# Weight sums of a Strassen product in six stages, a tile of its own for the first product, output weights in halves, and earlier requests for the reload and the first heads

## The chip, the cores and the metric

The kernel runs on one core of one Trainium2 chip. A core has TensorE (PE, matrix products), VectorE (DVE), ScalarE (ACT), GpSimd (POOL) and SyncE (SP, which mostly issues transfers), each with its own instruction stream that it works off in order, and DMA engines that move data between the chip's memory and the core's buffers. The engines wait for each other by semaphores. The metric is the device time of one execution in microseconds (us); lower is better.

## The reference

What is computed is one layer of a diffusion transformer: 2048 tokens on a grid 64 wide, and 256 context tokens, 1024 values each. One wide projection gives queries, keys, values and gates of a neighbourhood attention and of a retention; their gated results go through an output projection.

```python
def reference(x, c, ctx, c_ctx, norm_g, w_ada, b_ada, w_in, na_rpb, ret_decay_fwd,
              ret_decay_bwd, ret_norm_g, w_out, final_norm_g):
...
        mod = jax.nn.silu(c) @ w_ada[i] + b_ada[i]
...
        shift, scale, gate = mod[:, None, :D], mod[:, None, D:2 * D], mod[:, None, 2 * D:]
...
        h_lat = _rmsnorm(x, norm_g[i]) * (1.0 + scale) + shift
        h_ctx = _rmsnorm(ctx, norm_g[i]) * (1.0 + scale_c) + shift_c
...
        y_lat, y_ctx = _mixer(h_lat, h_ctx, w_in[i], na_rpb[i], lg_f, lg_b, ret_norm_g[i],
                              w_out[i], update_ctx)
        x = x + gate * y_lat
...
    return _rmsnorm(x, final_norm_g)
```

`_mixer` begins with the products `h @ w_in` (1024 x 4096) and ends with `@ w_out` (1024 x 1024). The kernel scales `w_out` by `gate` beforehand, and so has the gated sum from one product.

All values are float32. A product of float32 matrices is made of three TensorE products of rounded parts: each operand is cut into a high part (`whi`, `hhi`: a cast to the type `fp32r`, on ACT) and a low part (`wlo`, `hlo`: the rest, by a subtraction on POOL or VectorE), and high x high, high x low and low x high are summed in PSUM.

## The kernel before

The tokens of `h` are four blocks of 512 columns (`blk[0]` to `blk[3]`), each kept as a high and a low tile; the context is `blk[4]`. The kernel runs through these stages on TensorE:

1. Five windows (`window(b)`, products on line L354): the attention's keys for the four token blocks and the context. The norm and the cutting of the blocks run beside them, by a table of steps, `PLAN`: an entry is the step of a window, the action and its arguments. The actions `'w'` and `'w2'` request the raw weights of the first two context products (four DMAs of `w_in` into the staging tile `st`, issued by SP on L176).
2. Units of the context (six of 48 products, L365) and values of blocks 0 and 1 (`values`, eight units of 48).
3. The first Strassen region: queries and gates of blocks 0 and 1. Each of six sets (`SETS`) takes a weight of 1024 x 256 and makes four outputs by seven products instead of eight (`w_set`; each product, `prod` on L625, is 12 matmuls of 512 columns). The products are called by their weight: A11, A12, S4, A22, S2, S3, S1. Sums of quarters of the weight (`s1` to `s4`) and of the blocks (`t1` to `t4`) are made beforehand.
4. Values of blocks 3 and 2, and the second region for these blocks. The two blocks' tiles were stored to memory (`spill_step`, L487) and are loaded back (`reload_parts`, L771).
5. A lead of 192 products for the retention's values, beside which the first head of the attention is loaded; then attention (L944 and on), retention and output projection, which the change leaves alone.

The weight's sums are written in `w_sums`: a list of functions, one for each of the four steps of the set before (`step(n)` calls `ahead[n]`). `cut` makes one part: a cast on ACT (L579) and a subtraction on POOL (L580); the sums are VectorE's (L587 to L590 and L595). In `w_set`, ACT copies the first product to half of tile `o3` (L653), since VectorE adds it to the second (L654) and to S2's (L660). `o3` is one tile with no second buffer, and its other half is an output that a DMA stores (`fin` and `store`, L150; `gS`, `ggS` and `qS` are the stored gates and queries). PSUM holds six tiles for the products, handed out in the order in which they come free.

In the gaps of the regions runs the preparation of the output weight, called from a list of `hooks`, four for a set. `wo_gate(k)` adds one piece of `w_ada` into the row `gacc` (L690) and requests the next 512 KB (`wraw`, L687), `wo_row` turns the row into all partitions by two matmuls (L697), and `wo_mul(k)` multiplies one eighth of `w_out` by it (L701), cuts it (ACT L705, POOL L706) into two tiles `g` and stores four pieces to `woS` one step later, from ACT's queue (L708). `load_w` requests the raw weight for the next sum (L176), and `w_split` cuts a whole weight (ACT L336, POOL or VectorE L338).

At the lead's beginning SP has `load_w`, and after it the first head's loads: `load_head` (`k<-kS`), `load_q` and `load_v` (`vt<-vB`).

## Time and profile before

| what | us |
|---|---|
| time, median of three | 1449.82 |
| lowest and highest | 1444.53, 1451.17 |
| profiled execution | 1451.75 |
| its span in the profile | 1450.0 |
| mean granted TensorE clock | 0.969 of full speed |

The page of the profile gives busy time for each engine and the span in 40 slices of 36 us. Digits are tenths busy; PEclk is the clock granted to TensorE.

```profile
PE   6989899889898787789999999999999999999997
...
DVE  5686147455576343427776777777663544444445
ACT  5454232233223233236555645555563133333332
POOL 4352244434335545335553534446443144544442
PEclk9999899999989898999999999999999999999999
```

TensorE is at 7 to 9 tenths in the slices of 165 to 650 us (the 5th to the 18th digit), where the change lies, and at 9 or more behind. A row of a timeline reads: start, length, engine, line, operation, what it writes from what it reads, and in brackets the idle time of that engine before it and what ended it. `SPq` and `ACTq` are SP's and ACT's queues, where a DMA is issued.

### The profile page before, as it was taken

Reading aid. Unit: us, or ns where it says so; the run is one execution under the profiler, and the core shown is the slowest. Engines: PE = TensorE matmul, PEld = TensorE weight load, DVE = VectorE, ACT = ScalarE, POOL = GpSimd, SP = SyncE. Lnnn points to the kernel's source line nnn. Section 1 sums busy time; section 2 is a strip of 40 time slices with the busy share of each in tenths; the row PEclk is TensorE's granted clock in tenths of the full one; section 3 lists DMA queues with packets and bytes.
Section 4 is the critical chain, followed back from the end, with each engine's and each line's share of the span. In section 5 each row is a group of like instructions: output and inputs, shape, how many; then the busy total and the mean of one; then the engine's idle time right before and its main releaser. Section 6 shows DMA issues by size and latency. Waiting matters only on the chain.

```text
span 1450.0 us, 23128 instructions
## 1 busy us (share of the span) xinstructions
PE 1338.7 (92%) x8236; PEld 1167.1 (80%) x8236; DVE 828.2 (57%) x1426; ACT 589.1 (41%) x1239; POOL 620.9 (43%) x585
## 2 busy tenths in 40 slices
PE   6989899889898787789999999999999999999997
PEld 2467799667697666679889988998999879888886
DVE  5686147455576343427776777777663544444445
ACT  5454232233223233236555645555563133333332
POOL 4352244434335545335553534446443144544442
PEclk9999899999989898999999999999999999999999
DMA  9448664577684645488677779988555898655533
GB/s 317 149 160 290 224 198 109 167 270 226 251 300 112 213 130 183 172 237 233 183 180 211 204 204 270 278 213 219 167 149 171 246 298 267 200 183 166 162 117 124
DMA packets 231765, 295.64 MB, mean 204 GB/s; under 512 B 17633, under 2 KB 172385, under 8 KB 230626
## 3 DMA queue, kind: packets, MB, share of 16 engines
q1 hardware_dynamic: 200322, 237.79, 55.7%
q10 hardware_dynamic: 31328, 56.37, 10.9%
q8 instruction: 66, 1.08, 0.3%
q14 instruction: 49, 0.40, 0.1%
HBM read 196.57 MB, written 97.52 MB: 203 GB/s over the span
## 4 chain that ended last, share of the span: by engine, by line
PE 44%; DMA 5%; DVE 4%; issue 3%; POOL 3%; ACT 2%; SPq 0%; ACTq 0%; POOLq 0%; DVEq 0%
PE mm L1383 10%; PE mm L365 10%; PE sS L944 5%; PE mm L354 4%; PE tr L971 3%; PE po L992 3%; PE tr L973 2%; PE po L994 2%; PE mm L1106 2%; DMA v<-rvS 1%; DMA k<-kS 1%; PE mm L1295 1%; PE mm L1294 1%; PE mm L1293 1%; PE mm L1274 1%
## 5 line engine op out<-in xcount | busy, mean ns | idle before, releaser
L365 PE MATMUL mm<-whi,hhi 128*128 128x256 f32 x768 | 226.8, 295 | 0.7 <-DMA hhi<-hS 0.5
L365 PE MATMUL mm<-whi,hlo 128*128 128x256 f32 x768 | 219.2, 285 | 4.3 <-DMA hlo<-hS 4.3
L365 PE MATMUL mm<-wlo,hhi 128*128 128x256 f32 x768 | 219.0, 285 | 1.7 <-POOL wlo L338 1.7
L975 ACT CAST pt<-tr 128x640 fp32r<-128x640 f32 (+1 forms) x128 | 95.7, 748 | 169.9 <-PE tr L973 167.5
L981 DVE TENSOR_TENSOR pt<-tr,pt 128x640 fp32r<-128x640 f32 (+1 forms) x128 | 114.0, 890 | 77.1 <-ACT pt L975 75.8
L365 PEld LDWEIGHTS mm<-whi,hlo 128*128 128x128 f32 x768 | 148.5, 193 | 5.4 <-DMA hlo<-hS 5.3
L964 POOL TENSOR_SCALAR sp<-sp,stt 128x640 f32<-128x640 f32 (+2 forms) x128 | 103.5, 811 | 112.9 <-DVE stt L963 77.9
L365 PEld LDWEIGHTS mm<-wlo,hhi 128*128 128x128 f32 x768 | 148.2, 193 | 2.1 <-POOL wlo L338 2.1
L365 PEld LDWEIGHTS mm<-whi,hhi 128*128 128x128 f32 x768 | 148.2, 193 | 1.7 <-ACT o L634 0.7
L625 PE MATMUL mm<-hhi,whi 128*128 128x512 f32 x336 | 107.5, 421 | 35.3 <-DVE o L660 27.5
L953 DVE CUSTOM_DVE_ANT_0 sp<-sS,nb 128x640 f32<-128x640 f32 (+2 forms) x128 | 105.6, 825 | 37.4 <-DMA nb<-in_rpb_t_dram 23.7
L338 POOL TENSOR_TENSOR wlo<-st,whi 128x256 fp32r<-128x256 f32 (+1 forms) x79 | 83.8, 1072 | 98.9 <-ACT whi L336 78.1
L958 ACT ACTIVATE sp<-sp,stt 128x640 f32<-128x640 f32 (+2 forms) x128 | 107.4, 839 | 27.6 <-DVE stt L953 26.5
L625 PEld LDWEIGHTS mm<-hhi,whi 128*128 128x128 f32 x336 | 67.4, 202 | 56.3 <-issue 30.3
L944 PE MATMUL sS<-k,q 128*128 128x256 f32 (+3 forms) x512 | 99.5, 316 | 12.4 <-DMA vt<-vB 7.0
L354 PE MATMUL mm<-hhi,whi 128*128 128x512 f32 x256 | 108.3, 423 | 0.0
L354 PE MATMUL mm<-hlo,whi 128*128 128x512 f32 x256 | 102.1, 399 | 5.8 <-DVE hlo L255 2.3
L354 PE MATMUL mm<-hhi,wlo 128*128 128x512 f32 x256 | 102.5, 400 | 0.2 <-DVE wlo L338 0.2
L580 POOL TENSOR_TENSOR whi<-st,whi 128x512 fp32r<-128x512 f32 x48 | 66.4, 1404 | 78.3 <-ACT whi L579 51.5
L944 PEld LDWEIGHTS sS<-k,q 128*128 128x128 f32 x512 | 83.6, 190 | 18.7 <-DVE stt L953 7.7
L1383 PE MATMUL mm<-wor,y 128*128 128x512 f32 x384 | 95.6, 398 | 1.3 <-DVE xt L1392 1.2
L1392 DVE TENSOR_TENSOR xt<-mm,xt 128x512 f32<-128x512 f32 x64 | 43.8, 687 | 85.0 <-PE mm L1383 79.5
(254 smaller groups left out, 3116.2 us busy)
## 6 DMA issues: line engine op xcount, KB each, us to landing
st<-in_w_in_dram SPq DMA_DIRECT2D x64, 512.0 KB
q<-qS SPq DMA_DIRECT2D x64, 256.0 KB
k<-kS SPq DMA_DIRECT2D x16, 576.0 KB
kS<-o SPq DMA_DIRECT2D x16, 512.0 KB
hS<-hhi SPq DMA_DIRECT2D x16, 512.0 KB
hS<-hlo SPq DMA_DIRECT2D x16, 512.0 KB
vB<-o SPq DMA_DIRECT2D x64, 128.0 KB
qS<-o ACTq DMA_DIRECT2D x16, 512.0 KB
```

The costliest lines, as they stand in the source:

```text
L338: eng.tensor_tensor(l, r, f(h), ALU.subtract)
L354: nc.tensor.matmul(pm[:, :n], ww[:, k, cs], h[:, k, :], start=(k == 0 and i == 0), stop=(k == KC - 1 and i == 2))
L365: nc.tensor.matmul(pm[:, t * WG:(t + 1) * WG], h[:, k, o:o + P], ww[:, k, :], start=(k == 0 and i == 0), stop=(k == KC - 1 and i == 2))
L580: nc.gpsimd.tensor_tensor(t[:, 1], r, f(t)[:, 0], ALU.subtract)
L625: nc.tensor.matmul(pm, ww[:, k, :], hh[:, k, :], start=(k == 0 and i == 0), stop=(k == KH - 1 and i == 2))
L944: nc.tensor.matmul(o, hd["q"][i][:, hl, j * P:(j + 1) * P], k, start=(hl == 0), stop=(hl == 1))
L953: nc.vector.tensor_tensor_reduce(T["sp"][:, :n], T["s"], nbz[big][:, o:o + n], -1.0, 3e38, ALU.add, ALU.min, T["st"][:, 0:1])
L958: nc.scalar.activation(sp[:, :n], sp[:, :n], AF.Exp, bias=st[:, 0:1], scale=-1.0, accum_out=st[:, 1:2])
L964: nc.gpsimd.tensor_scalar(sp[:, :n], sp[:, :n], st[:, 2:3], 0.0, ALU.mult, ALU.add)
L975: nc.scalar.copy(pt[:, :ng_ + 2, 0, :], tr[:, :ng_ + 2, :])
L981: nc.vector.tensor_tensor(pt[:, :n, 1, :], tr[:, :n, :], f(pt)[:, :n, 0, :], ALU.subtract)
L1383: nc.tensor.matmul(pm, yy[:, k, :], ww[:, k, sl], start=(k == 0 and i == 0), stop=(k == 3 and i == 2))
```

## The change

It has seven parts:

- `PLAN`: the action `'w2'` (the second context weight) moves from step 106 to the end of window 3 (127).
- `w_sums`: four stages become six. The sums stand a stage after the first cuts, `a22` is cut a stage ahead of `s4`, `s3` ahead of `s2`, `s1` alone, and `load_w` last. Stages 0 to 3 run in the set before, stages 4 and 5 in the set's own first two steps (`mine[4 + n:5 + n] + ahead[n:n + 1]`), and `values` calls stages 0 to 2 after units 4, 5 and 6 and stage 3 at its end.
- `w_set`: the first product goes to the tile `e` (of the pool `wo["p"]`, one buffer), which also takes the sum `u3`; no DMA reads it. `o3` is first written at S2. After S1 the sum for `o3` comes first, and its `fin` too.
- `wo_open` runs ahead of the first region, `wo_gate(k)` at hooks 3k + 2 for k up to 6, `wo_gate(7)` after unit 1 of the second values, and `wo_row` after unit 7.
- `wo_mul(k, n)` does half n of piece k, at hook 3k + n, with a tile `g` of one buffer in place of two; the next load comes after the second half.
- The reload of blocks 3 and 2 is requested at hooks 20 and 21 (the first two steps of the region's last set).
- `load_w` stands behind the first head's loads.

```diff
-    (90, 'cs', 8), (92, 'rs', 8), (94, 'hl', 7, 0), (95, 'hl', 7, 1), (96, 'sp', 8), (106, 'w'), (106, 'w2'),
-    (108, 'mu', 8, 1), (108, 'ab', 8, 1), (109, 'hl', 8, 1), (114, 'mu', 8, 0), (117, 'ab', 8, 0), (127, 'hl', 8, 0),
+    (90, 'cs', 8), (92, 'rs', 8), (94, 'hl', 7, 0), (95, 'hl', 7, 1), (96, 'sp', 8), (106, 'w'),
+    (108, 'mu', 8, 1), (108, 'ab', 8, 1), (109, 'hl', 8, 1), (114, 'mu', 8, 0), (117, 'ab', 8, 0), (127, 'hl', 8, 0), (127, 'w2'),
...
         def p0():
             cut("a11", 0, 0, a11)
             cut("a12", 0, 1, a12)
+
+        def p1():
             V(a11, a11, a21, ALU.subtract)
             V(a12, a12, a22, ALU.subtract)
             V(a12, a12, a11, ALU.add)
             V(a21, a21, a22, ALU.add)
-
-        def p1():
+            cut("a22", 1, 1, a22)
+
+        def p2():
             cut("s4", 1, 0, a12)
-            cut("a22", 1, 1, a22)
             V(a22, a22, a11, ALU.subtract)
 
-        def p2():
+        def p3():
+            cut("s3", 2, 1, a11)
             cut("s2", 2, 0, a22)
-            cut("s3", 2, 1, a11)
-
-        def p3():
+
+        def p4():
             cut("s1", 3, 0, a21)
-            load_w()
-
-        return W, [p0, p1, p2, p3]
+
+        return W, [p0, p1, p2, p3, p4, load_w]
...
-        (oa, (_, xa)), (ob, (yb, xb)) = out_tile(), out_tile(True)
-        nc.scalar.copy(yb, prod(W["a11"], b11))
-        V(xa, prod(W["a12"], b21), yb, ALU.add)
+        et = wo["p"].tile([P, 2, 512], F32, name="e")
+        s1, u3 = (lay(et[:, e, :]) for e in range(2))
+        oa, xa = out_tile()
+        nc.scalar.copy(s1, prod(W["a11"], b11))
+        V(xa, prod(W["a12"], b21), s1, ALU.add)
         step(0)
         m3 = prod(W["s4"], b22)
         fin(oa, 0, A)
         m4 = prod(W["a22"], t4)
         step(1)
-        V(xb, prod(W["s2"], t2), yb, ALU.add)
-        V(yb, prod(W["s3"], t3), xb, ALU.add)
+        ob, xb = out_tile(True)
+        V(xb, prod(W["s2"], t2), s1, ALU.add)
+        V(u3, prod(W["s3"], t3), xb, ALU.add)
...
-        V(xd, m5, yb, ALU.add)
         V(xb, m5, xb, ALU.add)
+        V(xd, m5, u3, ALU.add)
+        fin(ob, 0, B)
         fin(od, 1, B)
-        fin(ob, 0, B)
         step(3)
...
-    def wo_mul(k):
-        nc.vector.tensor_tensor(wo["w"], wo["w"], wo["acc"], ALU.mult)
-        for n in range(2):
-            sl = slice(n * 512, (n + 1) * 512)
-            w = wo["p"].tile([P, 2, 512], F32R, name="g", bufs=2)
+    def wo_mul(k, n):
+        sl = slice(n * 512, (n + 1) * 512)
+        nc.vector.tensor_tensor(wo["w"][:, sl], wo["w"][:, sl], wo["acc"][:, sl], ALU.mult)
+        w = wo["p"].tile([P, 2, 512], F32R, name="g")
...
-        if k + 1 < KC:
+        if n == 1 and k + 1 < KC:
             wo_load(a["w_out"][(k + 1) * P:(k + 2) * P, :])
...
-    W = values((w0, w1), (0, 1), h_sums(T, 0, 1), None)
+    W, mine = values((w0, w1), (0, 1), h_sums(T, 0, 1), {})
+    wo_open()
+
+    def take(b):
+        for d in reload_parts(b):
+            nc.sync.dma_start(*d)
+
     hooks = [[spill_step] if n < 16 else [] for n in range(24)]
-    for n, e in enumerate([wo_open] + [g(k) for k in range(8)]):
-        hooks[2 * n + 1].append(e)
-    hooks[22].append(wo_row)
+    for k in range(7):
+        hooks[3 * k + 2].append(lambda k=k: wo_gate(k))
+    hooks[20].insert(0, lambda: take(3))
+    hooks[21].insert(0, lambda: take(2))
...
-    strassen(T, 0, 1, W, hooks, mid)
-    for b in (3, 2):
-        for d in reload_parts(b):
-            nc.sync.dma_start(*d)
+    strassen(T, 0, 1, W, mine, hooks, mid)
...
-    W = values((w0, w1), (3, 2), h_sums(T, 2, 3), None)
+    W, mine = values((w0, w1), (3, 2), h_sums(T, 2, 3), {1: lambda: wo_gate(7), 7: wo_row})
     hooks = [[] for n in range(24)]
     for k in range(8):
-        hooks[3 * k].append(m(k))
+        for n in range(2):
+            hooks[3 * k + n].append(lambda k=k, n=n: wo_mul(k, n))
...
-    load_w()
...
     heads[0] = load_head(0)
     load_q(heads[0], 0, 0)
     load_v(heads[0], (0, 1, 2))
+    load_w()
```

SP, in the last third of window 3, where the table's entry has moved; `hS` and `kS` are stores of a token block and of the keys, `st` the weight's staging tile.

```order
 L487 DMA hS_0_93<-hhi 128x1024 x2
 L150 DMA kS_61<-o 256x1x512
-L176 DMA st<-in_w_in_dram 128x4x256 x4
+L176 DMA st<-in_w_in_dram 128x4x256 x2
 L487 DMA hS_0_93<-hhi 128x1024 x2
 L150 DMA kS_62<-o 256x1x512
 L487 DMA hS_1_94<-hlo 128x1024 x2
 L150 DMA kS_63<-o 256x1x512
-L487 DMA hS_1_94<-hlo 128x1024 x2
+L487 DMA hS_1_94<-hlo 128x1024
+L176 DMA st<-in_w_in_dram 128x4x256 x2
+L487 DMA hS_1_94<-hlo 128x1024
```

Two of the four pieces now stand behind five stores of blocks and two of keys.

VectorE in one set of the first region, before; L654 adds the copy to A12's product, L595 is `a22` less `a11`, L660 takes S2's product:

```order
L654 TENSOR_TENSOR o<-mm,o_2495 128x512
L587 TENSOR_TENSOR st<-st 128x4x128
L588 TENSOR_TENSOR st<-st 128x4x128
L589 TENSOR_TENSOR st<-st 128x4x128
L590 TENSOR_TENSOR st<-st 128x4x128
L595 TENSOR_TENSOR st<-st 128x4x128
L690 SCALAR_TENSOR_TENSOR gacc<-wraw,silc,gacc 128x1024
L660 TENSOR_TENSOR o_2495<-mm,o_2495 128x512
L661 TENSOR_TENSOR o_2495<-mm,o_2495 128x512
```

and the same set now (L658 was L654, L665 was L660, L597 was L595, L695 was L690):

```order
L658 TENSOR_TENSOR o<-mm,e 128x512
L695 SCALAR_TENSOR_TENSOR gacc<-wraw,silc,gacc 128x1024
L589 TENSOR_TENSOR st<-st 128x4x128
L590 TENSOR_TENSOR st<-st 128x4x128
L591 TENSOR_TENSOR st<-st 128x4x128
L592 TENSOR_TENSOR st<-st 128x4x128
L665 TENSOR_TENSOR o_2568<-mm,e 128x512
L666 TENSOR_TENSOR e<-mm,o_2568 128x512
L668 TENSOR_TENSOR o<-mm,e 128x512
L669 TENSOR_TENSOR o_2568<-mm,o_2568 128x512
L597 TENSOR_TENSOR st<-st 128x4x128
L674 TENSOR_TENSOR o_2568<-mm,o_2568 128x512
```

The subtraction of `a22` has moved from ahead of S2's add to behind four adds, and the gate's sum from behind the weight's sums to ahead of them.

ACT in the first set of the second region, before; `g` is the cut of the output weight and `woS` its store, L639 and L150 a gate and its store, L579 a cast of the weight's sums:

```order
L653 COPY o_3652<-mm 128x512
L579 CAST whi<-st 128x512 x2
L705 CAST g<-wraw 128x512 x2
L639 ACTIVATE o<-o 128x512
L708 DMA woS_95<-g 128x512
L708 DMA woS_96<-g 128x512
L708 DMA woS_95<-g 128x512
L708 DMA woS_96<-g 128x512
L150 DMA gS_69<-o 128x512
```

and now (L657 was L653, L709 was L705, L712 was L708):

```order
L657 COPY e<-mm 128x512
L579 CAST wlo<-st 128x512
L579 CAST whi<-st 128x512 x2
L709 CAST g<-wraw 128x512
L640 ACTIVATE o<-o 128x512
L712 DMA woS_95<-g 128x512
L712 DMA woS_96<-g 128x512
L150 DMA gS_69<-o 128x512
L579 CAST wlo<-st 128x512
L709 CAST g<-wraw 128x512
L640 ACTIVATE o<-o 128x512
L712 DMA woS_95<-g 128x512
```

The second cast of `g` stands behind the stores of the first, and both write the same tile.

More of the change, by code (lines that the diff above doesn't have):

```diff
@@ L609, in p1, with w_set @@
             res.append(w_split(wcur.pop(0), lo=1))
-        return [None, p1, None, None]
-    def w_set(c0, W, T, A, B, ahead, hooks):
+        return [None, p1, None, None, None, None]
+    def w_set(c0, W, T, A, B, mine, ahead, hooks):
         isq = c0 < 512
@@ L629, in out_tile @@
             o = env["st"].tile([P, 2, 512], F32R, name="o3", bufs=1) if extra else op.tile([P, 2, 512], F32R, name="o")
-            return o, [lay(f(o)[:, e, :]) for e in range(2)]
+            return o, lay(f(o)[:, 1, :])
         def fin(o, ct, b):
@@ L644, in step @@
             tick()
-            if ahead[n]:
-                ahead[n]()
+            for fn in mine[4 + n:5 + n] + ahead[n:n + 1]:
+                if fn:
+                    fn()
             if hooks:
@@ L717, in unit, with strassen @@
             spill_step()
-    def strassen(T, A, B, W, hook, last):
+    def strassen(T, A, B, W, mine, hook, last):
         for n, c0 in enumerate(SETS):
@@ L724, in strassen, with values @@
                 Wn, ahead = last, plain_next(last)
-            w_set(c0, W, T, A, B, ahead, hook)
-            W = Wn
-    def values(ws, bb, hs, W):
-        ahead = [None] * 4
+            w_set(c0, W, T, A, B, mine, ahead, hook)
+            W, mine = Wn, ahead
+    def values(ws, bb, hs, hook):
         vu = [(w, c0, tp) for w, c0 in zip(ws, (1024, 1280)) for b in bb for tp in (2 * b, 2 * b + 1)]
@@ L738, in values @@
             if n == 4:
-                W, ahead = w_sums(wcur.pop(0))
-            if n in (4, 5):
-                ahead[n - 4]()
+                W, mine = w_sums(wcur.pop(0))
+            if n > 3 and n < 7:
+                mine[n - 4]()
+            if n in hook:
+                hook[n]()
         while hs:
             hs.pop(0)()
-        ahead[2]()
-        ahead[3]()
-        return W
+        mine[3]()
+        return W, mine
     load_w()
```

22 lines of the change are left out of this document (10 added, 12 removed).

## The prediction

> **What bounds the kernel now.** The page says first how the whole run stands: its busy rows and the clock.
>
> ```profile
> span 1450.0 us, 23128 instructions
> PE 1338.7 (92%) x8236; PEld 1167.1 (80%) x8236; DVE 828.2 (57%) x1426; ACT 589.1 (41%) x1239; POOL 620.9 (43%) x585
> ```
>
> TensorE is the bound on average, with some 110 us idle. An average tells nothing of a stage, so I cut the span at the borders that the timeline shows (context and first values, first Strassen region, second values, second Strassen region, lead to the attention) and asked for busy time by stage. Columns: stretch, its length, busy time and instructions of each engine, granted clock, DMA share, GB/s.
>
> ```profile
> 165.50:256.30 90.80, 83.81 (x672) 83.51 (x673) 48.77 (x40) 27.62 (x37) 38.42 (x17) 0.94 0.55 163
> 256.30:393.30 137.00, 124.23 (x511) 98.05 (x510) 70.33 (x87) 42.40 (x74) 58.28 (x43) 0.96 0.68 222
> 393.30:450.70 57.40, 51.82 (x385) 49.72 (x383) 44.99 (x36) 15.24 (x22) 22.04 (x10) 0.91 0.75 254
> 450.70:613.70 163.00, 128.75 (x504) 100.70 (x505) 66.78 (x88) 50.44 (x89) 77.14 (x60) 0.90 0.54 171
> 613.70:645.90 32.20, 23.74 (x193) 23.09 (x191) 10.52 (x12) 8.86 (x14) 10.75 (x11) 0.96 0.72 214
> ```
>
> The two regions have 504 products each (the 511 are with those of `wo_row`), and take 137 and 163 us. No engine is full in them; what TensorE waits for there is named by its waits from 165 to 650 us (total, times, longest):
>
> ```profile
> PE mm L625 <- DVE o L660: 27.5, 7, 7.9
> PE mm L625 <- ACT o L653: 9.1, 2, 5.8
> PE sS L944 <- DMA vt<-vB: 7.0, 1, 7.0
> ```
>
> L660 is the VectorE add that empties product S2's PSUM buffer. VectorE's own waits from 250 to 650 us say why it comes late:
>
> ```profile
> DVE o L654 <- ACT o L653: 65.9, 10, 13.6
> DVE st L595 <- POOL wlo L580: 44.7, 12, 7.9
> ```
>
> It stands before L654 until ACT has copied the set's first product (L653), and before L595 until POOL has cut `a22` (L580), and only then reaches L660. The copy itself waits for a store of the tile it writes, and then TensorE waits:
>
> ```profile
> 298.53 0.59 ACT L653 COPY o<-mm 128x512 f32<-128x512 f32 x1 [4.86 <-DMA gS<-o]
> 284.36 0.47 PE L625 MATMUL mm<-hhi,whi 128*128 128x512 f32 x1 [3.69 <-DVE o L660]
> ```
>
> **The floor.** Two stretches without a wait, at clock 1.00, give the price of a product: 20.00/169 = 0.1183 us at 256 columns, 20.00/88 = 0.2273 us at 512.
>
> ```profile
> 220.00:240.00 20.00, 20.00 (x169) 20.00 (x169) 15.59 (x11) 5.16 (x6) 7.15 (x3) 1.00 0.50 123
> 320.00:340.00 20.00, 20.00 (x88) 16.25 (x87) 12.24 (x14) 6.27 (x12) 9.87 (x7) 1.00 0.75 256
> ```
>
> So the five stages cannot be under 672 × 0.1183 = 79.5, 504 × 0.2273 = 114.5, 384 × 0.1183 = 45.4, again 114.5, and 192 × 0.1183 = 22.7 us. `wo_row` adds 1.9 (137.0 holds it now; after the change it stands in the second values). Together 378.5, against 480.4 measured and 1.3 of slow products behind the last wait (below), 481.7. **The most this change can gain is 103.2 us.** Everything after is untouched. I now say, stage by stage, what wait is left.
>
> **(a) The second context weight.** SP is in order. At 139 us it takes the four pieces of the two context weights and stands in them until POOL has split a piece of the context and so freed the staging tile (the second row is SP's waits from 136 to 176 us).
>
> ```profile
> 139.24 13.67 SPq L176 DMA_DIRECT2D st<-in_w_in_dram  x4
> SPq L176 <- POOL clo L271: 11.2, 2, 7.6
> 169.49 0.37 ACT L374 CAST o<-mm 128x256 fp32r<-128x256 f32 x1 [3.31 <-DMA kS<-o]
> 169.76 1.99 ACT L336 CAST whi<-st 128x1024 fp32r<-128x1024 f32 x2
> 173.29 0.58 PE L365 MATMUL mm<-wlo,chi 128*128 128x256 f32 x1 [1.64 <-POOL wlo L338]
> 170.00:180.00 10.00, 7.50 (x36) 7.21 (x37) 2.66 (x4) 4.29 (x6) 8.02 (x3) 0.54 0.58 184
> ```
>
> The `kS` stores of the windows queue behind it, ACT's evictions (L374) wait for those stores' tiles, and the first weight's cast (L336) stands behind them on ACT. TensorE, done with the windows at 165.5, so runs steadily from 173.3 only (7.8 us), and then at a clock of 0.54: 36 products in 7.50 us, where 4.3 is their price (3.2). With two pieces moved behind the stores, SP passes that place earlier by the one wait that goes with them, 7.6 at most and 11.2 − 7.6 = 3.6 at least; the stores, the evictions and the cast move up by as much. By 7.6 the cast ends at 164.2, ahead of the windows' end; by 3.6 TensorE still waits 4.2. I take the first, since POOL's two splits follow each other and the later one is what the moved pieces wait for, and leave 0.8 for POOL's low part. The moved weight is wanted a unit later (48 × 0.1183 = 5.7 us, 171 us), some 18 us after the 153 us at which SP is through with it even now. 90.8 → 80.3.
>
> **(b), (c) Six stages and tile `e`.** The number of cuts and sums is the same; they are spread over more steps of 19.1/4 = 4.8 us each (7 × 12 × 0.2273 = 19.1 a set). `a22`'s cut now precedes L595's subtraction by a whole step, which takes away the 44.7; the copy goes to a tile that no DMA reads, which takes away most of the 65.9. The wait for `o3`'s store is not gone: it moves to the add of S2's product, four products or 10.9 us into the set, where the store, asked for at the end of the set before, has landed unless it takes over twice the 4.86. A new wait is that `e` must be free of the set before, whose last reader is the add of S1's product; queued behind the copy on ACT are cuts of later steps. VectorE does that add while TensorE has 12 × 0.2273 = 2.7 us of A11: nothing, as long as VectorE is no further behind. Sums of the first set now run during values, where VectorE is behind already:
>
> ```profile
> 267.31 1.29 DVE L404 TENSOR_TENSOR o<-mm,o 128x512 fp32r<-128x512 f32 x2 [1.17 <-ACT o L403]
> ```
>
> That is the last unit's work, done at 268.6, while TensorE left the unit at 256.3. The first set's cut of `s4` stands some way ahead of it and is wanted 5.5 us into the region; bounds 0 and 268.6 − 261.8 = 6.8. I take 1.7, since only one unit's additions (about half of the lag) stand behind the cut, and 1.0 for the rest of the region. `wo_open` moves ahead of the region with a memset and two requests, beside TensorE's work: nothing. 137.0 − 1.9 → 117.2.
>
> **(d), (f) The reload.** Before, its sixteen parts are requested from 385 us on; the products meet them coming in.
>
> ```profile
> 385.16 0.50 SPq L771 DMA_DIRECT2D hhi<-hS  x1
> 409.56 0.32 SPq L771 DMA_DIRECT2D hlo<-hS  x1
> 397.10 0.38 PE L365 MATMUL mm<-whi,hlo 128*128 128x256 f32 x1 [2.00 <-DMA hlo<-hS]
> ```
>
> The parts take 24.4 us from first to last issue. Asked for in steps 0 and 1 of the last set, about 14 and 10 us before that set ends, block 3 (twelve or so us) is there when the units start, and block 2's last part lands about 10 us into them, before the unit that reads it (half of 45.4 us). What stands behind them on SP is a weight load and hidden by the same time. I leave 0.6 for a part that shares the queues. `wo_gate(7)` and `wo_row` add one 1.7 us VectorE operation and 1.9 us of TensorE. 57.4 → 45.4 + 1.9 + 0.6 = 47.9.
>
> **(e) The output weight in halves.** This is where I am least sure. There is one `g` tile now, so a chain closes on itself: multiply half, cast, POOL's subtraction, two stores, their landing, cast of the second half, subtraction, load of the next weight, landing. Before, over the second region (busy us, mean ns, idle before):
>
> ```profile
> L706 POOL TENSOR_TENSOR g<-wraw,g 128x512 fp32r<-128x512 f32 x14 | 18.6, 1352 | 12.3 <-issue 7.0 <-ACT g L705 5.2
> L705 ACT CAST g<-wraw 128x512 fp32r<-128x512 f32 x14 | 8.0, 616 | 18.1 <-DVE wraw L701 18.1
> L701 DVE TENSOR_TENSOR wraw<-wraw,gacc 128x1024 f32<-128x1024 f32 x7 | 8.5, 1217 | 0.0
> 492.49 0.85 ACTq L150 DMA_DIRECT2D gS<-o  x2
> 496.45 0.59 ACT L653 COPY o<-mm 128x512 f32<-128x512 f32 x1 [1.42 <-DMA gS<-o]
> 496.48 2.71 ACTq L708 DMA_DIRECT2D woS<-g  x4
> 290.00 0.34 SPq L687 DMA_DIRECT2D wraw<-in_w_ada_dram  x1
> 294.46 1.66 DVE L690 SCALAR_TENSOR_TENSOR gacc<-wraw,silc,gacc 128x1024 f32<-128x1024 f32 x1 [3.44 <-DMA wraw<-in_w_ada_dram]
> ```
>
> Multiply 0.6, cast 0.6, subtraction 1.35, two issues 1.36, then 3.5 to landing (a 256 KB `gS` store: second issue near 492.95, free at 496.45), cast 0.6, subtraction 1.35, load 4.5 (290.00 to 294.46, 512 KB): 13.9 us, of which 8.0 are landings and 5.9 work. Three steps are 14.3 us. That is even, and the stores wait for the next step's start and stand in ACT's order with the evictions; so I take about 1 us a weight of delay that reaches TensorE, 8 us. Bounds: nothing (covered), and 8 × 3.5 = 28 where ACT's whole wait for the landing reaches it. While ACT waits, queued behind are the set's copy, cuts and gate evictions, and VectorE after them. The start of the region is again late for `s4`, 3.7 us here (the values are paced by TensorE with no slack for VectorE's 45 us of 57). 114.5 + 11.7 = 126.2 in place of 163.0.
>
> The Trainium skill's page "DMA: Bandwidth & Descriptors" (Anatomy of one DMA) gives each transfer about 2.0 us fixed plus its bytes at 436 GB/s, for the path issued by GpSimd, most of it the receipt of the write. An estimate by it is 2.6 us for a store here and 3.2 for a load, against 3.5 and 4.5 in the rows; the chain would be 11.7 us, well within three steps, and the time 8 us lower, 1358. The rows decide. The same rule speaks against halves with one buffer, as the fixed part is paid in the chain twice.
>
> **(g) Heads before the weight.** Before, SP stood at the weight until POOL freed its tile, and then the head's keys and values were requested; these are rows of the chain that ended last, and TensorE's rows behind it:
>
> ```profile
> 625.78 4.76 POOL wlo L338 x2
> 632.15 10.35 DMA k<-kS
> 642.52 3.31 DMA vt<-vB
> 645.94 1.24 PE L944 MATMUL sS<-k,q 128*128 128x288 f32 x4 [7.03 <-DMA vt<-vB]
> 646.98 0.41 PE L365 MATMUL mm<-whi,hhi 128*128 128x256 f32 x1
> 649.54 1.03 PE L944 MATMUL sS<-k,q 128*128 128x384 f32 x4
> ```
>
> The heads' transfers take 10.35 + 3.31 = 13.7 us, and without the wait for POOL they start near the lead's beginning, under 22.7 us of products. Left 0.3; the weight behind them is needed after the lead's products only. The twelve products behind the 7.03 us gap take 649.54 − 646.98 = 2.6 us where 12 × 0.1183 = 1.4 is the price: a gap of that length costs 1.2 to 1.3 more. That goes: 32.2 + 1.3 → 23.0. But one gap of such a length may be left in the second region (3.7 at its start with what follows), so I add 1.3 there.
>
> The Trainium skill's page "TensorE: Matmul & The Clock Gate" (Part 1) has the clock halved after an idle window of about 3.4 us, and as long to return; the rows agree (0.21 us a product until 649.5, 3.6 us after the start). By it, eight waits of 1 us cost no more than themselves, and without my added term the sum would be 1364.6.
>
> **Sum.** After: 80.3 + 117.2 + 47.9 + 126.2 + 23.0 + 1.3 = 395.9, against 481.7: 85.8 less. The profiled execution took 1451.75 (span 1450.0 and 1.75 around it): **1366**. It stands 1.9 above the median of 1449.82, which is within what the runs scatter.
>
> **The rivals.**
> *A, the weight's chain sets the pace of region two.* For: 13.9 against 14.3 us leaves nothing, and any extra wait recurs eight times. Against: each landing must be slower than the rows. At 17.5 us a weight (two landings of 5.8) the region is 8 × 17.5 = 140, 14 more: 1380; at 20.6 it is 165, like today's 163: 1405. Chance 0.16.
> *B, the requests gain nothing.* The reload's and heads' transfers, asked for earlier, collide with spills and stores (DMA share 0.75 and 0.72), and TensorE waits as before. Gives back 9.5 and 10.5: 1376 to 1386. Chance 0.09.
> *C, VectorE stays late for L660's successor.* The sums are as many, and POOL's cuts slow VectorE beside them. Then the regions' 17.9 and 36.8 don't come: 1366 + 54.7 = 1421. Against it: VectorE is busy for 70.33 of 137 us. Chance 0.05.
> *D, slower: the single `g` tile holds ACT for two slow landings at each weight.* To cancel 85.8, region two must last 212 us, 26.5 a weight; less 5.9 of work that is landings of 10.3 each, where the slowest row, for two 576 KB loads, is 10.35. From there on it is slower, at 28 us 1452 + 12 = 1464. Chance 0.03.
> *E, nothing changes,* since the tile `e` or the earlier requests end up behind the same waits: 1450. Chance 0.01.
>
> **How the numbers follow.** The forecast, 1352 to 1380, has 0.64; 0.02 is for less than 1352 (no more than 3.4 us of waits above the floor of 1348.6). The range 1352 to 1400 holds the forecast, B and three quarters of A (0.12): 0.85. It reaches over the bounds of (a), up to 1370, of (b), 1364 and 1371, and of (e), 1358 and 1386. About 0.5% (7 us) is what a measurement of this kernel can tell from no change. Faster by more: 0.64 + 0.02 + 0.16 + 0.09 + 0.05 = 0.96; same 0.01; slower 0.03.
>
> **What would show it.** (a): TensorE's first product of L365 within 2 us of the windows' end. (b), (c): no wait of the copy for a `gS` store, the row L595's successor has for POOL near zero, the first region near 117. (d), (f): no `hlo<-hS` among TensorE's waits. (e): the second region near 126; if it is 140 or more with ACT's cast of `g` waiting for `woS`, A holds. (g): no wait of the first attention product for `vt`. The forecast is wrong if the second region stays over 140, or if TensorE's waits for VectorE's emptying of S2 stay above 10 us.

## The result, and the profile after

The changed kernel takes 1392.17 us (median of four, 1387.76 to 1392.92) against 1448.58 (four runs of before): a ratio of 0.9607, interval 0.9576 to 0.9638. That is 56 us less, where 1366 was forecast, 26 less than measured. The profiled execution took 1392.92 us, its span is 1391.1, and the mean granted clock 0.984 (0.969 before). The same stages as before, cut where TensorE changes from one kind of product to the next:

```profile
162.85:244.62 81.77, 81.13 (x675) 80.73 (x674) 48.10 (x36) 25.27 (x34) 37.28 (x17) 1.00 0.57 165
244.62:368.75 124.13, 119.71 (x506) 96.50 (x505) 75.73 (x91) 43.16 (x75) 60.98 (x43) 0.97 0.75 251
368.75:425.00 56.25, 52.44 (x389) 50.24 (x388) 42.68 (x35) 14.31 (x19) 24.09 (x11) 0.91 0.77 251
425.00:557.30 132.30, 122.80 (x507) 95.52 (x506) 76.89 (x93) 52.00 (x90) 80.02 (x58) 0.97 0.63 204
557.30:587.87 30.57, 24.81 (x194) 24.61 (x193) 9.51 (x13) 6.57 (x10) 8.35 (x10) 0.89 0.94 294
```

| stage | before | forecast | after |
|---|---|---|---|
| context and first values | 90.8 | 80.3 | 81.8 |
| first region | 137.0 | 117.2 | 124.1 |
| second values with `wo_row` | 57.4 | 47.9 | 56.3 |
| second region | 163.0 | 126.2 + 1.3 | 132.3 |
| lead (before: with 1.3 of slow products) | 32.2 + 1.3 | 23.0 | 30.6 |
| sum | 481.7 | 395.9 | 425.1 |

The miss is 29 us in these stages, a little of which came back elsewhere (the windows ended 2.65 us sooner). Four stages are 5 to 8 us longer than forecast; the second values and the lead gained only some 3 us each (the 1.9 of `wo_row` stood in the first region before). TensorE's waits from 150 to 620 us have new names:

```profile
PE mm L626 <- ACT wlo L579: 8.4, 3, 4.8
PE mm L365 <- ACT o L440: 5.8, 1, 5.8
PE mm L626 <- POOL wlo L580: 4.3, 6, 1.3
PE mm L365 <- DMA hlo<-hS: 3.3, 4, 0.9
PE mm L626 <- POOL whi L580: 1.0, 2, 0.9
PE mm L365 <- POOL wlo L338: 0.6, 1, 0.6
```

Gone are the waits for the add of S2 (27.5) and for the copy (9.1), for the attention's `vt` (7.0) and for the first context weight (5.4). In their place: the cuts of the weight's sums on ACT and POOL (L579, L580; the longest are of `s4`, at the regions' starts), a copy in the lead (L440), and the reload nearly as before (3.3 us, 4.3 before). VectorE's two long waits are answered too, from 240 us on:

```profile
DVE o L658 <- ACT e L657: 17.2, 6, 5.6
...
DVE st L589 <- POOL whi L580: 15.8, 6, 4.8
```

The add of A12 waits 17.2 us for the copy where it waited 65.9, and the subtraction of `a22` (now L597) is not among the waits any more (44.7 before). L589 is the set's first sum, whose wait for POOL is about what it was (17.2 before, as L587). The add of A12 also waits for stores and for its product, so that its waits come to 40.2 us, against 79.4.

The three places where TensorE waits, in the order of time. At the first region's start, ACT's order: the cut of `s4` (third row) stands behind the cut of a block's sum, which waited 6.03 us for VectorE, and TensorE had nothing to do from 250.25 us on.

```profile
251.70 0.62 ACT L524 CAST hhi<-o 128x512 fp32r<-128x512 f32 x1 [6.03 <-DVE o L564]
252.22 0.58 ACT L403 CAST o<-mm 128x512 fp32r<-128x512 f32 x1
252.70 0.62 ACT L579 CAST wlo<-st 128x512 fp32r<-128x512 f32 x1
```

Before the second values, SP's queue (the length of an issue is the time SP stood in it):

```profile
354.98 0.34 SPq L769 DMA_DIRECT2D hhi<-hS  x1
...
358.67 0.34 SPq L769 DMA_DIRECT2D hlo<-hS  x1
360.39 0.33 SPq L692 DMA_DIRECT2D wraw<-in_w_ada_dram  x1
362.97 5.35 SPq L176 DMA_DIRECT2D st<-in_w_in_dram  x2
368.41 0.46 SPq L769 DMA_DIRECT2D hhi<-hS  x1
```

Block 3 is requested from 355 us on, but block 2 only from 368.41, behind a weight for which SP stands 5.35 us, when the region is over. But the order on SP is not all of it: the DMA engines are full from the first request on (their share is the number before the last).

```profile
355.00:368.75 13.75, 13.75 (x60) 11.11 (x59) 10.02 (x9) 3.89 (x6) 6.36 (x4) 1.00 0.99 359
368.75:390.00 21.25, 17.44 (x119) 15.96 (x118) 14.71 (x12) 5.20 (x7) 9.05 (x3) 0.85 1.04 399
```

In these 35 us they move 13.4 MB, of which the reload is 8.4 (sixteen parts of 512 KB); weights and the stores of the queries are most of the rest. SP's longest wait at that weight, 4.5 us, is put down to such a store. TensorE's last wait for block 2 ends at 389.3 us, 20.6 us into the values.

In the lead, ACT again (a cast of the output weight waits for the store of the half before, from the tile `g` that both use):

```profile
568.58 0.62 ACT L709 CAST g<-wraw 128x512 fp32r<-128x512 f32 x1 [6.73 <-DMA woS<-g]
...
572.20 1.99 ACT L336 CAST whi<-st 128x1024 fp32r<-128x1024 f32 x2 [1.95 <-DMA vt<-vB]
574.10 0.58 ACT L440 COPY o<-mm 128x512 f32<-128x512 f32 x1
```

Behind that cast stands the copy (L440) that empties the PSUM tile TensorE waits for.

### The profile page after: what moved, and what is told of

The parts are those of the page before. It is cut to its first block, busy times and chain, and to the rows that moved or that the text cites. A ratio compares the mean times of both kernels' runs of the same rounds, so it can differ in the third digit from the quotient of the medians.

```text
span 1391.1 us, 23111 instructions
## 1 busy us (share of the span) xinstructions
PE 1323.0 (95%) x8236; PEld 1157.6 (83%) x8236; DVE 840.3 (60%) x1434; ACT 591.0 (42%) x1239; POOL 627.1 (45%) x585
## 4 chain that ended last, share of the span: by engine, by line
PE 46%; DVE 4%; DMA 2%; ACT 2%; issue 1%; POOL 1%; SPq 0%; ACTq 0%; POOLq 0%; DVEq 0%
PE mm L1390 11%; PE mm L365 10%; PE sS L950 5%; PE mm L354 4%; PE tr L977 3%; PE po L998 3%; PE tr L979 2%; PE mm L1113 2%; PE po L1000 2%; DMA v<-rvS 1%; PE mm L1302 1%; PE mm L1301 1%; PE mm L1300 1%; PE mm L1281 1%; DVE xt L1358 1%
## 5 line engine op out<-in xcount | busy, mean ns | idle before, releaser
L354 PE MATMUL mm<-hhi,whi 128*128 128x512 f32 x256 | 107.6, 420 | 0.0
L626 PE MATMUL mm<-hhi,whi 128*128 128x512 f32 x336 | 98.4, 395 | 1.2 <-POOL whi L580 1.0
L1390 PE MATMUL mm<-won,y 128*128 128x512 f32 x336 | 89.9, 406 | 0.0
L1390 PEld LDWEIGHTS mm<-wor,y 128*128 128x128 f32 x384 | 69.9, 188 | 17.1 <-issue 3.5
```

Of the source, the lines that this page charges most:

```text
L354: nc.tensor.matmul(pm[:, :n], ww[:, k, cs], h[:, k, :], start=(k == 0 and i == 0), stop=(k == KC - 1 and i == 2))
L626: nc.tensor.matmul(pm, ww[:, k, :], hh[:, k, :], start=(k == 0 and i == 0), stop=(k == KH - 1 and i == 2))
L1390: nc.tensor.matmul(pm, yy[:, k, :], ww[:, k, sl], start=(k == 0 and i == 0), stop=(k == 3 and i == 2))
```

## The experiments

Each is the changed kernel with one edit, unless said otherwise; each time is a median beside runs of the kernel before on the same chip, with the ratio to these and its interval.

### Undoing one part

**The second context weight back at step 106:**

```diff
-    (106, 'w'),
+    (106, 'w'), (106, 'w2'),
```

> The changed kernel with only the second context weight's request put back to step 106. Theory 1 (its own stall counts in full, with the low clock behind it): the idle 7.8 us and 3.2 us at half clock before the context's products come back, 10 to 13 us more, 1402 to 1405. Rival (the stores behind it were late for another reason, or a later wait absorbs it): within 3 us of 1392.

1401.29 us, 0.9673 (0.9656 to 0.9691), 9 more. TensorE's old wait is back:

```profile
168.64 0.58 PE L365 MATMUL mm<-whi,chi 128*128 128x256 f32 x1 [5.05 <-ACT whi L336]
171.07 0.58 PE L365 MATMUL mm<-wlo,chi 128*128 128x256 f32 x1 [1.64 <-POOL wlo L338]
```

So this part was priced about right: 10.5 forecast, 9 measured.

**The reload after the region:**

```diff
-    hooks[20].insert(0, lambda: take(3))
-    hooks[21].insert(0, lambda: take(2))
...
     strassen(T, 0, 1, W, mine, hooks, mid)
+    take(3)
+    take(2)
```

> The changed kernel with both blocks' reload requested after the first region again. By my prediction's step the early request is worth 9 us: 1401. Theory 1 (in the changed kernel block 2 is still requested from 368 us only, behind a weight's load on SP, so that little was gained): 2 to 5 us more, 1394 to 1397. Rival (requesting early costs by contention): 1392 or less.

1392.37 us, 0.9610 (0.9591 to 0.9629): no difference that can be told. The second values take 58.4 us in place of 56.3, and the second region 128.9 in place of 132.3. What the early request brings in one stage is gone in the next; it is not worth 9 us, nor the 2 to 5 of Theory 1.

**The weight ahead of the heads:**

```diff
     wseq += [c0 for _, c0 in fseq[2:]]
+    load_w()
...
     load_v(heads[0], (0, 1, 2))
-    load_w()
```

> The changed kernel with the weight's load ahead of the first head's loads again. By my prediction's step the order is worth 10 us: 1402. Theory 1 (the early heads now collide with the last stores of the output weight, and ACT waits for these, so most of the gain was given back): 2 to 6 us more, 1394 to 1398. Rival (the heads are no longer late in either order): within 2 us of 1392.

1395.83 us, 0.9629 (0.9602 to 0.9655): 3 to 4 more, though the intervals overlap. The lead now shows the wait that the change removed, and not the one that it brought (1.3 us for L440 in place of 5.8):

```profile
589.87 1.25 PE L951 MATMUL sS<-k,q 128*128 128x288 f32 x4 [6.54 <-DMA vt<-vB]
```

One wait of 6 to 7 us was exchanged for another. That is where the 10 us went. Why the new wait is there in the changed kernel only is in ACT's row for the last cast of `g`, which waits for the same store:

```profile
565.41 0.62 ACT L709 CAST g<-wraw 128x512 fp32r<-128x512 f32 x1 [2.29 <-DMA woS<-g]
```

It waits 2.29 us where it waited 6.73. Here SP stands at the weight, the heads' loads come only from 576 us on, and the cast goes on 2.9 us after the store's first issue; in the changed kernel the loads run beside the store, and it takes 7.4. So the early requests slow the store.

**The first product in `o3` again, six stages kept:**

```diff
-        et = wo["p"].tile([P, 2, 512], F32, name="e")
-        s1, u3 = (lay(et[:, e, :]) for e in range(2))
-        oa, xa = out_tile()
+        (oa, (_, xa)), (ob, (yb, xb)) = out_tile(), out_tile(True)
+        s1 = u3 = yb
...
-        ob, xb = out_tile(True)
```

> The changed kernel with the first product copied to the stored tile o3 again, six stages kept. Theory 1 (both the tile and the stages are needed): TensorE's waits for the add of S2's product return, 10 to 25 us more, 1402 to 1417. Rival (the stages alone do it): within 5 us of 1392.

1409.22 us, 0.9720 (0.9695 to 0.9746), 17 more. The edit also puts back the order of the last two adds and of their outputs, so the price is that of both.

**Four stages again, tile `e` kept:**

```diff
-        return W, [p0, p1, p2, p3, p4, load_w]
+        return W, [p0, p1, p2, p3, None, None]
```

(the functions as before the change)

> The changed kernel with four stages of weight sums as before, the tile e kept. Theory 1 (both are needed): the cut of a22 again stands just ahead of its subtraction, TensorE waits for the add of S2, and s4's cut is late in every set; 10 to 25 us more, 1402 to 1417. Rival (the tile alone does it): within 5 us of 1392.

1402.29 us, 0.9682 (0.9656 to 0.9709), 10 more. In its profile (an execution of 1406.70) the loss is in the second region (146.0 us for 132.3); the first is no longer than with six stages (122.9 for 124.1). **Both undone together**, the two edits above in one kernel:

> The changed kernel with the copy into o3 and the four stages both put back. Undone alone they cost 17 and 10 us against 1392. If they act apart: 1417 to 1421. Theory 1 (one wait of TensorE for the add of S2, which either half of the change can leave standing in part): 1425 to 1440, with TensorE's waits for that add at 20 us or more, since w2, heads and reload explain only some 13 of the 56 us.

1434.11 us, 0.9899 (0.9860 to 0.9938), 42 more, where 17 + 10 would be 27. The regions take 136.9 and 158.4 us, nearly as before (137.0 and 163.0), and the wait for the add of S2 is back, at 17.1 us and not the 20 that were expected:

```profile
PE mm L625 <- DVE o L662: 17.1, 5, 5.1
```

With one half kept this wait is small (1.1 us with the six stages, 7.0 with the tile). VectorE's waits from 240 to 650 us say why, in the kernel with `o3`, in the one with four stages, and in the one with both undone:

```profile
DVE o L657 <- ACT o L656: 48.8, 9, 10.2
```

```profile
DVE st L595 <- POOL wlo L580: 44.9, 12, 6.2
```

```profile
DVE o L656 <- ACT o L655: 68.5, 10, 13.3
DVE st L595 <- POOL wlo L580: 44.8, 12, 6.2
```

Each half holds off one of the two long waits that stood ahead of the add of S2 (65.9 and 44.7 us before the change). With either of them alone VectorE still reaches the add almost in time, with both it doesn't. So read from the kernel without either, the tile alone brings 32 us (1434.1 to 1402.3), the stages alone 25 (to 1409.2), and the second of them, on top of the first, only 10 or 17. What makes up these 17 and 10 us is less clear: TensorE's longest wait with `o3` is for the cut of the weight's sums on ACT (11.1 us, 8.4 in the changed kernel), and with four stages one that is put down to the cast of the output weight (10.8 us); I did not follow them further.

The parts undone here come to some 55 of the 56 us (42, 9 for the context weight, 3 to 4 for the heads, nothing for the reload). The halves of the output weight and the gate's new places were not undone; the sum leaves little for them on balance.

### Mending one place

**Block 2's reload ahead of the weight** in the same step, so that its first part is requested 6 us sooner (362.2 for 368.4) and its last 3 us (376.6 for 379.6):

```diff
         def step(n):
             tick()
+            if hooks and 24 - len(hooks) in first:
+                first.pop(24 - len(hooks))()
             for fn in mine[4 + n:5 + n] + ahead[n:n + 1]:
...
-    hooks[21].insert(0, lambda: take(2))
+    first[21] = lambda: take(2)
```

> The changed kernel with block 2's reload ahead of the weight's load in the same step. Theory 1 (the waits of 3.8 us for block 2 and about 5 us at half clock come from the request behind the weight): block 2 is requested from about 361 us, 6 to 9 us less, 1383 to 1386. Rival (the transfers are limited by bandwidth, not by their request): not more than 3 us less, with the same waits for hlo.

1406.90 us, 0.9718 (0.9695 to 0.9741): 15 us slower; neither theory had that. The weights are late instead:

```profile
378.36 13.60 SPq L176 DMA_DIRECT2D st<-in_w_in_dram  x6
386.93 1.04 ACT L336 CAST whi<-st 128x1024 fp32r<-128x1024 f32 x1 [17.07 <-DMA st<-in_w_in_dram]
436.10 0.80 PE L626 MATMUL mm<-hhi,whi 128*128 128x512 f32 x1 [14.61 <-ACT whi L579]
```

(SP, ACT, TensorE.) The values themselves are some 3 us shorter, and TensorE's waits for the reload fall from 3.8 to 2.4 us; the DMA engines are as full as before (a share of 0.99 and 1.03 from 355 to 380 us). But SP comes to the weights at 378 us. ACT waits 17 us for one; behind it, on ACT and on VectorE, stand the blocks' sums and behind these the cut of the region's first operand, so that TensorE runs through the values and then waits 14.61 us for the first product, A11. With the engines full, what the reload gains the weights lose, and the second region hangs on the chain of weight, cast and sums that has to be done by the end of the values.

**The stages of each region's first weight one unit of values earlier:**

```diff
-            if n == 4:
+            if n == 3:
                 W, mine = w_sums(wcur.pop(0))
-            if n > 3 and n < 7:
-                mine[n - 4]()
+            if n > 2 and n < 7:
+                mine[n - 3]()
...
-        mine[3]()
```

> The changed kernel with the stages of a region's first weight one unit of values earlier (after units 3 to 6). Theory 1 (s4's cut stands behind the blocks' sums in ACT's and VectorE's order, and each of the two waits costs its length and some 4 us at half clock): 10 to 18 us less, 1374 to 1382. Rival (VectorE is late as a whole, so that the blocks' sums or the values' evictions are late in its place): not more than 4 us less.

1392.25 us, 0.9614 (0.9586 to 0.9641): no difference. In its profile the first region is shorter, 118.9 us for 124.1, but the second is 133.5 for 132.3: the wait at its start is 1.8 us instead of 5.6, and others come later in it. The profiled execution is the fastest of the four (1388.46 us, the slowest 1394.99). So the theory holds for the waits that it names, and a gain in the total is not shown.

**Tiles of 128 x 512 with three buffers for the cut output weight**, and one half tile for `e`, so that they fit:

```diff
-        et = wo["p"].tile([P, 2, 512], F32, name="e")
-        s1, u3 = (lay(et[:, e, :]) for e in range(2))
+        s1 = u3 = lay(wo["p"].tile([P, 512], F32, name="e"))
...
-        w = wo["p"].tile([P, 2, 512], F32R, name="g")
-        nc.scalar.copy(w[:, 0, :], wo["w"][:, sl])
-        nc.gpsimd.tensor_tensor(w[:, 1, :], wo["w"][:, sl], f(w)[:, 0, :], ALU.subtract)
+        w = [wo["p"].tile([P, 512], F32R, name="g", bufs=3) for hl in range(2)]
+        nc.scalar.copy(w[0], wo["w"][:, sl])
+        nc.gpsimd.tensor_tensor(w[1], wo["w"][:, sl], f(w[0]), ALU.subtract)
```

> The changed kernel with the cut output weight in tiles of 128x512 with three buffers, and e in one half tile so that it fits. Theory 1 (the wait of 5.76 us in the lead is ACT's cast waiting for the last store of g, and the clock falls behind it): 6 to 9 us less, 1383 to 1386. Rival (the transfers of the heads set the lead's end, or ACT waits elsewhere): not more than 2 us less.

1389.01 us, 0.9595 (0.9566 to 0.9623), 3 less, which the intervals don't tell apart. The cast no longer waits, but the wait has only moved one row on, to the issue of the store in ACT's queue:

```profile
561.48 0.62 ACT L708 CAST g<-wraw 128x512 fp32r<-128x512 f32 x1 [1.36 <-DVE wraw L706]
...
562.68 4.92 ACTq L711 DMA_DIRECT2D woS<-g  x2
...
570.56 0.58 ACT L440 COPY o<-mm 128x512 f32<-128x512 f32 x1
```

### Measuring two disputed prices

**The clock behind a wait**, by products that fill it:

```diff
         step(0)
+        if warm and c0 == SETS[0]:
+            pm = ptile(psm)
+            for k in range(warm.pop(0)):
+                nc.tensor.matmul(pm, W["a11"][:, 0][:, k % KH, :], b11[0][:, k % KH, :], start=True, stop=True)
         m3 = prod(W["s4"], b22)
...
+        if n == 1:
+            for k in range(44):
+                nc.tensor.matmul(sS[:, 0:256], blk[3][0][:, k % KC, 0:P], blk[3][0][:, k % KC, 0:256], start=True, stop=True)
```

> The changed kernel with products that nobody reads put where TensorE waits: 13 of 512 columns ahead of S4 in the first set of region one, 20 in region two, 44 of 256 columns after the lead's second unit. They add work (13 x 0.2273, 20 x 0.2273 and 44 x 0.1183: 12.7 us) and take no wait away. Theory 1 (behind each wait some 2 to 5 us are lost to the halved clock): the clock stays at 1.00 behind these three places, and the time falls by 6 to 12 us, 1380 to 1386. Rival (the waits alone cost, or the next wait takes up what TensorE does sooner): 1390 to 1398.

1390.72 us, 0.9607 (0.9577 to 0.9637): no difference. By stage it divides. Where the products fell into the wait the clock stayed up: the first region takes 121.7 in place of 124.1, the lead 28.3 in place of 30.6, 2.4 and 2.3 us saved by added work. The stretch behind the first region's wait, of the changed kernel and then of this one (the clock is the third number from the right):

```profile
255.00:260.00 5.00, 4.60 (x11) 3.64 (x12) 0.89 (x1) 1.91 (x4) 5.00 (x5) 0.50 0.85 213
```

```profile
255.00:260.00 5.00, 3.69 (x16) 2.71 (x17) 2.21 (x3) 3.40 (x7) 5.00 (x5) 1.00 0.73 163
```

In the second region the products were put badly: they write the PSUM tile of `wo_row`, so they waited 5.1 us for ACT themselves and then ran for 4.5 us on top; that stage took 135.5 in place of 132.3. So a wait of that size costs some 2 us more than its length. The changed kernel's own rows agree: behind the first wait 12 products take 5.2 us (without the wait of 1.29 between them) where 2.7 is their price, and in the lead 16 take 3.55 where 1.9 is. The total of this run shows nothing; its third place lost 3.2 of the 4.7 us that the other two won.

**The output weight's chain**, left out (the sixteen stores stay, all from the one half that is still cut):

```diff
     def wo_mul(k, n):
         sl = slice(n * 512, (n + 1) * 512)
+        if k == 0 and n == 0:
...
-        if n == 1 and k + 1 < KC:
-            wo_load(a["w_out"][(k + 1) * P:(k + 2) * P, :])
```

> The changed kernel without the chain of the output weight: one half of one piece is multiplied and cut, and stored as all sixteen; the other fifteen multiplications, cuts and loads are left out. By my prediction's term the chain costs region two 8 us: 1384; with the lead's wait for its last store and the clock behind it (5.8 and 2): 1376. Rival (the chain is hidden, region two's short waits are those of POOL's cuts of the weight sums, and the lead is held by the heads' transfers): within 4 us of 1392.

1380.70 us, 0.9535 (0.9503 to 0.9566), 11.5 less. The second region and the lead:

```profile
428.00:554.60 126.60, 120.01 (x504) 96.50 (x503) 72.12 (x86) 45.09 (x78) 61.04 (x45) 0.96 0.62 197
554.60:578.00 23.40, 23.40 (x197) 23.40 (x195) 3.47 (x6) 5.06 (x8) 5.80 (x7) 1.00 1.04 322
```

From product to product the region takes 127.2 us, 5.1 less than the changed kernel, and the lead 23.0, 7.6 less: its floor (22.7) with the heads' transfers running through it at a share of 1.04. So the heads' transfers don't hold the lead up by themselves. What holds it in the changed kernel is the end of the chain on ACT, which waits for a store that these transfers slow (above, the weight ahead of the heads).

### A version from this

The chain three steps earlier, and only the first region's stages one unit earlier:

```diff
...
+    hooks[23].append(lambda: wo_gate(7))
...
-    W, mine = values((w0, w1), (3, 2), h_sums(T, 2, 3), {1: lambda: wo_gate(7), 7: wo_row})
+    W, mine = values((w0, w1), (3, 2), h_sums(T, 2, 3), {1: wo_row, 2: lambda: wo_mul(0, 0), 4: lambda: wo_mul(0, 1)})
...
-    for k in range(8):
+    for k in range(1, 8):
         for n in range(2):
-            hooks[3 * k + n].append(lambda k=k, n=n: wo_mul(k, n))
+            hooks[3 * (k - 1) + n].append(lambda k=k, n=n: wo_mul(k, n))
```

> The changed kernel with the output weight's chain three steps earlier (the last gate piece in region one's last step, the row after unit 1 of the second values, the first two halves after units 2 and 4, and each further half three steps sooner), so that its last store is issued before the lead, and region one's weight stages one unit earlier. Theory 1 (the lead's 7 us are ACT's wait at the end of that chain, region one's 5 us the late cut of s4): lead at 23 to 25 us, region one at 119, total 1378 to 1384. Rival (the chain's work in the second values makes s4's cut in region two later by as much, or the heads' transfers hold the lead anyway): 1387 to 1393.

1385.03 us (median of five, 1383.37 to 1389.85), 0.9560 (0.9544 to 0.9577). It is below both kernels; against the changed one's 0.9576 to 0.9638 the intervals just meet, so 7 us are likely and not certain. The profiled execution is the slowest of the five. Both theories have a part in it:

```profile
PE mm L626 <- ACT wlo L579: 8.4, 2, 7.9
PE mm L626 <- POOL wlo L580: 4.3, 8, 0.8
...
PE mm L365 <- ACT o L440: 1.2, 1, 1.2
```

The lead is 24.5 us (30.6) and the first region 120.0 (124.1), as Theory 1 had it; and the wait at the second region's start has grown from 4.8 to 7.9 us, as its rival had it, since the chain's first halves stand in the second values: that region takes 136.7.

## Why the prediction was right and wrong

What held: TensorE's idle time was the bound, the floor was the right ruler, the direction and the two main sources were right. The range (1352 to 1400) holds 1392; the forecast's own range (to 1380) doesn't, and 1392 is also above what rival B gave (to 1386). It lies in the part that was taken in for rival A, which did not come: that the range holds it is partly luck.

- **(a)** "90.8 → 80.3": 81.8, and 9 us when undone. Right.
- **(b), (c)** The mechanism was right, and shown by undoing both: 42 us, with VectorE's two waits and TensorE's wait for S2's add back. (The two rows that the prediction shows for it, the copy at 298.53 and TensorE's wait at 284.36, don't belong to one wait: TensorE's is the earlier.) The term left standing was mis-sized. "I take 1.7" for the first cut of `s4`, within bounds of 0 and 6.8: it was 3.1 and 1.3 us of wait, and the clock after it. In the second region 3.7 was taken, and it was 4.8 and 0.8.
- **(d), (f)** "57.4 → 47.9": 56.3. The step that failed is "block 2's last part lands about 10 us into them": TensorE waited for it until 20.6 us into them. I took the 24.4 us from first to last issue as the time of the requests, and they were that of full DMA engines (a share of 1.01 to 1.03 from 390 to 415 us in the kernel before). An estimate from the rows of the changed kernel: at 359 to 399 GB/s the reload's 8.4 MB take 21 to 23 us with nothing beside them, from 355 us on until 376 to 378, and 5 MB of other transfers went in the same stretch. SP's order added to it: step 1 is 8.2 us before the set's end by the prediction's own prices and not 10, and SP meets the weight of the same step there, for which it stood 5.35 us. And a second step was missing: the weights, casts and blocks' sums on ACT and VectorE are done no sooner than the values, so that even a later reload (58.4 us) is made up in the region behind (128.9).
- **(e)** "about 1 us a weight of delay that reaches TensorE, 8 us": the region without the chain is 5.1 us shorter, so the term was near in the region. What the sum left out is the chain's end: without the chain the lead is 7.6 us shorter.
- **(g)** "32.2 + 1.3 → 23.0": 30.6. The wait for `vt` went, as forecast, and ACT's wait for the last store, which the early loads slowed, took its place. I had asked what stands behind the casts on ACT within the region, and not in the lead, where only two PSUM tiles are left for the products.
- **The clock.** I added 1.3 us for one gap. Of the 425.0 us, TensorE is busy for 400.9, and its products' price is 378.5: 22.4 us are busy time above the price, where 1.3 were forecast; idle are 24.1, where 16.1 were. So of the 29 us missed, 21 are busy time above the price and 8 waits. An estimate from the granted clocks of the stages (each stage's length times what its clock lacks of 1.00) puts at most some 16 us of this to the clock. The filled waits show 2.4 and 2.3 us each; for the short waits of the second values and of the second region's sets, the part that is clock and the part that is the pipeline filling again was not measured apart.

Of the rivals, B came closest, "the requests gain nothing", in both stages that it names, and in part for its reason. In the lead the heads' loads do collide with a store (6.73 us of wait, 2.29 without them), and the single tile `g` and ACT's order hand that on to TensorE. In the second values the DMA engines are full, and SP's order adds to it. Its price of 20 us is 16.0 here (8.4 and 7.6 above forecast). A did not come: the second region is at 132, not 140. C is refuted by the waits: none is for the add of S2 now. D's mechanism, ACT held by the single `g`, was seen four times, for 9.0 us in all, of which 6.73 are the one in the lead.

The sentence on the Trainium skill's page "DMA: Bandwidth & Descriptors" would have made the chain shorter than the rows did; the last store shows the opposite, with ACT waiting 6.73 us for 256 KB while the heads load (a share of 0.94 in that stage). With the heads later it was 2.9 us from issue to the end of the wait, near the 2.6 of the prediction's estimate by the Trainium skill.

## What to carry to other kernels

Where two waits stand ahead of one step, undoing one part at a time understates both: 10 and 17 us apart, 42 together, so undo them together too. When a transfer is asked for earlier, read in its new place the row ahead of it in the queue and the share of the DMA engines: where that is near 1, it can only change places with another, and the one that it overtakes may be the one that binds (15 us lost by letting a reload pass a weight). Where work is cut into a chain with one buffer, price its last link in the stage behind, not only its pace.

## What was not expected of the hardware

The granted clock fell to half without a long wait. In the second values, TensorE's five waits from 381 to 390 us are 0.91 us at the longest, yet:

```profile
380.00:385.00 5.00, 2.64 (x15) 2.03 (x14) 4.12 (x2) 0.74 (x1) 3.14 (x1) 0.87 1.02 414
385.00:390.00 5.00, 3.55 (x13) 2.68 (x13) 4.18 (x4) 1.13 (x3) 0.00 (x0) 0.50 1.06 376
390.00:395.00 5.00, 5.00 (x29) 5.00 (x29) 3.58 (x3) 1.31 (x2) 0.00 (x0) 0.61 1.07 360
395.00:400.00 5.00, 5.00 (x44) 5.00 (x43) 4.05 (x3) 0.91 (x2) 2.40 (x1) 1.00 0.60 139
```

Busy for 2.64 and 3.55 of 5 us, it was at half clock from 384 to 393.8 us, 4.4 us beyond the end of its last wait (29 products in 5 us instead of 44). The Trainium skill's page "TensorE: Matmul & The Clock Gate" (Part 1, What's actually happening) ties the half clock to an idle window of about 3.4 us; its part on psum-queue depth-cycling tells of short idle times that do the same. This trace agrees with the second. The prediction went by the first ("eight waits of 1 us cost no more than themselves"), and these rows show that it doesn't hold where the waits are close together; for waits a weight (14 us) apart, as the prediction meant them, they show nothing.
